# Padding the on-chip tiles that matmuls read to multiples of 128 bytes, in a fused two-block transformer kernel

## The chip, the cores and the metric

The kernel runs on one core of one Trainium2 chip. The metric is the device time of one execution in microseconds, as the median of several runs. The profiled execution, from which all durations here come, is one more run, recorded by the hardware profiler; its own time and its span from the first to the last instruction are given beside the median.

## The reference

Two different transformer blocks are applied one after the other to `x`, 256 tokens of 1024 features, each block two layers deep. All arrays are float32. What matters here is that nearly all the work is matrix products of 256 or 512 token columns with large weight matrices:

```python
# block 1, each of 2 layers
h = rms_norm(x, norm_mix_pre); proj = h @ w_in          # convolution, retention, gated linear attention
x = x + rms_norm(merged @ w_out, norm_mix_post)
f = (silu(h @ w_gate) * (h @ w_up)) @ w_down
x = x + rms_norm(f, norm_ffn_post)
# block 2, each of 2 layers: 256 latent tokens x and 256 context tokens, modulated by silu(c) @ ada_w
mix_x, mix_c = token_mixers(hx, hc, ...)                # conformer convolution, mLSTM, attention
x = x + g1 * mix_x
x = x + g2 * conv_ffn(hx, ffn_w_up, ..., ffn_w_down)    # the context too, in the first layer
```

## The kernel before, in words

Activations are kept with the features on the partitions and the tokens along the row, 128 features to a tile. Weights come from one long stream in DRAM, in the order of use, in chunks of 128 partitions by at most 1024 values (`load`, `chunk`). A float32 product is made from three products of type fp32r: `halve` splits each chunk of weights into a high part `whi` (ScalarE, L197) and a low part `wlo` (VectorE, L199); the activations are split in the same way. `mmT` (L214, L218, L220) then issues high by high, low by high and high by low, with 128 columns of the weights loaded into TensorE and 256 or 512 token columns streamed through (PSUM tiles `pj`, `dn`, `br`). `mmK` (L228, L230, L232) does the reverse where tokens are wanted on the partitions (PSUM tile `pk`): 128 token columns of the activations are loaded and the weights are streamed, 256 columns at a time, or 272 where 16 gate columns ride along (`tok_gates`, `tok_gates_first`). So `whi` and `wlo` are the loaded operand in `mmT` and the streamed one in `mmK`. Small products in plain fp32 (transposes, attention scores, sums of squares, retention and gated attention: `st`, `ro`, `go`, `ms`, `pv` and others) make up the rest; each of those leaves two records in the trace.

All tiles come from pools, laid out in SBUF in the order in which `setup` makes them, each tile rounded up to 32 bytes per partition. The first byte of the constants is 1,152, nine times 128. Where the program's own list of addresses puts the tiles, modulo 128:

| Pool (tile sizes in bytes per partition) | Start modulo 128 | Read by matmuls as |
|---|---|---|
| `pc`, constants: `vecs` 2716, `mats` 512, `sel` 288, `twice` 144, `hb` 96 and others | 0, 32, 64 or 96 | operands of small fp32 products |
| `pw`: `raw`, `whi`, `wlo` (4096) | 64 | weights of all large products |
| `psm`: 11 small tiles (64) | 0 or 64 | column scales in `rsb` |
| `ph`, `pu`, `pt`, `pg` (2048): `hh`, `hl`, `xh`, `xl`, `yl` and most others | 0 | activations |
| `pv`: 5 tiles of 2 x 258 (2064) | 32, 64, 96, 0, 32 | `v` of the mLSTM, some of `yh`, `xh` of `b2_first` |
| `pkc`, `pp`, `pz`, `pg2` (2048, 2304, 1024) | 64 (two of `pg2` at 0) | `kc`, some of `yh`, `fh`, `fl`, `fah`, `fal` |

In a chunk of 272 columns the parts follow each other at 1088 bytes, so they start at 64, 0 and 64. In the stretch at 1537 us the six `yh` tiles of a group lie at 32, 0, 32, 64, 64 and 64, and the six `yl` tiles at 0. By the same list the fp32r matmuls of 256 columns are 10,799 with the streamed operand at 0 and the loaded one at 64; 1,168 with 64 and 0; 1,024 with the streamed one at 32 or 64 (or in the midst of such) and the loaded one at 64; and 24 small ones. Of 512 columns there are 2,368 and 536 with the streamed operand at 0 and not; of 272 columns 288, of 258 columns 64.

The order of the matmuls is the order in which the program issues them; splits and loads run ahead of their use by a priority (`PRE_SPLIT`, `PRE_DMA`), as far as the four buffers of `whi` and `wlo` and the five of `raw` allow.

Of the kernel before, what the change touches and what calls it, by code (L numbers as in the profile page):

```python
# [8 lines left out]
F32 = mybir.dt.float32  # L9
F32R = mybir.dt.float32r  # L10
# [92 lines left out]
class Kern:  # L103
# [84 lines left out]
            (queue or self.nc.sync).dma_start(raw, self.d[stream][at : at + 128 * n].rearrange("(p n) -> p n", p=128))  # L188
        return raw

    def halve(self, raw, n, after=None):

        nc = self.nc
        with self.tc.high_priority(offset=self.PRE_SPLIT):
            hi = self.p_w.tile([128, 1024], F32R, tag="whi", name=self.nm("whi"))[:, 0:n]
            lo = self.p_w.tile([128, 1024], F32R, tag="wlo", name=self.nm("wlo"))[:, 0:n]
            self.high = nc.scalar.activation(hi, raw, AF.Copy)  # L197
            with self.tc.issue_after(after.ins) if after else nullcontext():
                self.mark = nc.vector.tensor_tensor(out=lo, in0=raw, in1=hi.bitcast(F32), op=ALU.subtract)  # L199
        return hi, lo  # L200

    def chunk(self, name, l, r0, kt, c0, width, after=None):
        n = kt * width
        self.ada_beat()
        raw = self.load(self.stream.add(name, l, r0, kt, c0, width), n)
        return [t.rearrange("p (k c) -> p k c", k=kt) for t in self.halve(raw, n, after)]

    def mmT(self, out, w, xh, xl, cs=slice(0, 128), first=True, last=True, mid=None):

# [91 lines left out]
    def setup(self, es):  # L301
        tc, nc, d = self.tc, self.nc, self.d
        MS = bass.MemoryType

        self.PRE_DMA, self.PRE_SPLIT, self.PRE_SOON, self.PRE_NORM = 600, 60, 150, 300
        self.p_c = es.enter_context(tc.tile_pool(name="pc", bufs=1))
        self.p_w = es.enter_context(tc.tile_pool(name="pw", bufs=4))
        self.p_s = es.enter_context(tc.tile_pool(name="psm", bufs=11))
        self.p_h = es.enter_context(tc.tile_pool(name="ph", bufs=12))
        self.p_u = es.enter_context(tc.tile_pool(name="pu", bufs=22))  # L310
        self.p_t = es.enter_context(tc.tile_pool(name="pt", bufs=7))
        self.p_g = es.enter_context(tc.tile_pool(name="pg", bufs=6))
        pool = lambda n, b: es.enter_context(tc.tile_pool(name=n, bufs=b))
        self.p_k = pool("pk", 1)
        self.p_v = pool("pv", 5)
        self.p_kc = pool("pkc", 4)
        self.p_p = pool("pp", 4)
        self.p_z = pool("pz", 2)
        self.p_g2 = pool("pg2", 2)
        self.p_ps = es.enter_context(tc.tile_pool(name="pps", bufs=3, space=MS.PSUM))  # L320
        self.p_aux = es.enter_context(tc.tile_pool(name="paux", bufs=3, space=MS.PSUM))
        self.p_pv = es.enter_context(tc.tile_pool(name="ppv", bufs=2, space=MS.PSUM))
        c = self.p_c
        self.xc = c.tile([128, 8, 512], F32, name="xc")
        self.vecs = c.tile([128, self.vec.n], F32, name="vecs")
        with tc.high_priority(offset=5000):
            for j in range(2):
                nc.sync.dma_start(self.xc[:, 4 * j : 4 * j + 4, 0:256], d["xT"][512 * j : 512 * j + 512].rearrange("(k p) t -> p k t", p=128))
            nc.scalar.dma_start(self.vecs[:, 0:8], d["vecs"][:, 0:8])
            if "b1" in self.parts:  # L330
                self.early = self.load(self.stream.add("w_in", 0, 0, 3, ((GV, 256), (GA, 16)), 272), 816, queue=nc.scalar)
        nc.scalar.dma_start(self.vecs[:, 8:], d["vecs"][:, 8:])
        self.mats = c.tile([128, 128], F32, name="mats")
        nc.scalar.dma_start(self.mats, d["ident"])
        self.ident = self.mats
        self.one256 = c.tile([128, 256], F32, name="one256")
        nc.gpsimd.memset(self.one256, 1.0)
        self.ones = self.one256[:, 0:128]
        self.mhalf = c.tile([128, 16], F32, name="mhalf")
        nc.gpsimd.memset(self.mhalf, -0.5)  # L340
        self.m1024 = c.tile([128, 2], F32, name="m1024")
        nc.gpsimd.memset(self.m1024, 1.0 / 1024)

        self.silu = c.tile([128, 2, 1024], F32, name="silu")
        self.mods = c.tile([128, 2, 48, 2], F32, name="mods")
# [747 lines left out]

    def b2_setup(self):
        nc, d, p = self.nc, self.d, self.p_c
        self.sel = p.tile([16, 2, 36], F32, name="sel")
        nc.scalar.dma_start(self.sel, d["sel"])
        self.cmask = p.tile([128, 2, 128], F32, name="cmask")
        nc.scalar.dma_start(self.cmask, d["cmask"])
        self.twice = p.tile([128, 36], F32R, name="twice")  # L1100
        nc.vector.tensor_tensor(out=self.twice, in0=self.ident[:, 0:36], in1=self.ident[:, 64:100], op=ALU.add)
        self.one1 = self.one256[0:36]
        self.m512 = p.tile([128, 2], F32, name="m512")
        nc.gpsimd.memset(self.m512, 1.0 / 512)
        self.tabs = p.tile([128, 2, 2, 2, 64], F32, name="tabs")
        self.m1 = p.tile([128, 2, 2, 8], F32, name="m1")
        self.hb = p.tile([128, 24], F32, name="hb")
        self.ctx = {}

    def b2_prep(self, l):  # L1110

        nc = self.nc
        V = nc.vector

        for i, (w, sc) in enumerate((("norm1", 8), ("norm2", 32))):
            for s in range(2):
                V.scalar_tensor_tensor(self.m1[:, i, s, :], self.mods[:, l, sc : sc + 8, s], 1.0, self.cols(f"{w}{l}"), ALU.add, ALU.mult)
        V.tensor_scalar(self.hb, self.cols(f"branch_gate_b{l}"), 0.5, None, ALU.mult)

        small = self.u("E")  # L1120
        nc.scalar.dma_start(small[:, 0:508], self.d["prep"][:, l])
        rope = small[:, 0:256].rearrange("p (c t d) -> p c t d", c=2, t=2)
        for i in range(2):
            w = small[:, 256 + 64 * i : 320 + 64 * i]
            V.tensor_tensor(out=self.tabs[:, i, 0], in0=rope[:, 0], in1=w[:, None, :].to_broadcast([128, 2, 64]), op=ALU.mult)
            for a, b in ((0, 32), (32, 0)):
                V.tensor_tensor(out=self.tabs[:, i, 1, :, a : a + 32], in0=rope[:, 1, :, a : a + 32], in1=w[:, None, b : b + 32].to_broadcast([128, 2, 32]), op=ALU.mult)
        V.tensor_scalar(self.tabs[:, 0], self.tabs[:, 0], 0.125, None, ALU.mult)

        k = lambda tag, n: self.p_k.tile([128, n], F32, tag=tag, name=self.nm(tag))  # L1130
        self.hw = k("hw", 124)
        V.tensor_scalar(self.hw, small[:, 384:508], 0.5, None, ALU.mult)
        self.hn = k("hn", 8)
        V.tensor_scalar(self.hn, self.cols(f"mlstm_norm{l}"), 0.5, None, ALU.mult)
        wr = k("wr", 128)
        V.tensor_scalar(wr[:, 0:64], small[:, 256:320], 0.125, None, ALU.mult)
        V.tensor_copy(wr[:, 64:128], small[:, 320:384])
        self.wrow = [wr[:, 0:64], wr[:, 64:128]]
# [435 lines left out]
    def mlstm_kv(self, l, S, h, gates=None):  # L1574


        nc = self.nc
        A = nc.scalar
        k = []
# [1 line left out]
            k.append(self.u("mk"))  # L1581
            A.activation(k[-1], ps, AF.Copy, scale=1.0 / 16)
        v = {}
        new = lambda: self.p_v.tile([128, 2, 258], F32, tag="v", name=self.nm("v"))
        if gates:
            ps = self.tok_gates("w_in_2", l, 3072, 1024 + 3072 + 1024, *self.feats(S), self.mm)
            gates(ps)
# [116 lines left out]
        return self.p_g.tile([128, 512], dt, tag="g", name=self.nm(name))  # L1704

    def vu(self, name, dt=F32):
        return self.p_v.tile([128, 2, 258], dt, tag="v", name=self.nm(name)).rearrange("p a b -> p (a b)")[:, 0:512]

    def b2_mixer(self, l, ahead):

# [164 lines left out]
    def b2_first(self, l, tiles):  # L1875
# [3 lines left out]
        H, L = [], []  # L1879
        with self.tc.high_priority(offset=self.PRE_NORM):  # L1880
            for j in range(4):
                hi = self.p_v.tile([128, 2, 258], F32R, tag="v", name=self.nm("xh"))
                sh = self.mods[:, l, 24 + 2 * j : 26 + 2 * j, 0:1]
                A.activation(hi[:, :, 256:257], sh, AF.Copy)
                V.tensor_tensor(out=hi[:, :, 257:258], in0=sh, in1=hi[:, :, 256:257].bitcast(F32), op=ALU.subtract)
                H += [hi[:, a] for a in range(2)]
                lo = self.bu("xl", F32R)
                L += [lo[:, a * 256 : a * 256 + 256] for a in range(2)]
            for k in range(8):
                A.activation(H[k][:, 0:256], self.xc[:, k, 0:256], AF.Copy, scale=self.m1[:, 1, 0, k : k + 1])  # L1890
            for k in range(8):
                V.scalar_tensor_tensor(L[k], self.xc[:, k, 0:256], self.m1[:, 1, 0, k : k + 1], H[k][:, 0:256].bitcast(F32), ALU.mult, ALU.subtract)
# [304 lines left out]
```

## Time and profile before

| | |
|---|---|
| median of 3 runs (lowest, highest) | 2542.06 us (2538.91, 2551.09) |
| profiled execution, its span | 2540.95 us, 2539.2 us |
| TensorE matmuls busy, weight loads busy | 98%, 91% of the span |
| VectorE, ScalarE, GpSimd busy | 75%, 51%, 6% |
| granted TensorE clock | 0.998 of full speed |

The share of busy time is an average over stages. TensorE's matmuls are pipelined: a record lasts longer than the time to the start of the next one, so how fast they follow each other is read from their starts.

### The profile page before, as it was taken

Reading aid. Unit: us, or ns where it says so; the run is one execution under the profiler, and the core shown is the slowest. Engines: PE = TensorE matmul, PEld = TensorE weight load, DVE = VectorE, ACT = ScalarE, POOL = GpSimd, SP = SyncE. Lnnn points to the kernel's source line nnn. Section 1 sums busy time; section 2 is a strip of 40 time slices with the busy share of each in tenths; the row PEclk is TensorE's granted clock in tenths of the full one; section 3 lists DMA queues with packets and bytes.
Section 4 is the critical chain, followed back from the end, with each engine's and each line's share of the span. In section 5 each row is a group of like instructions: output and inputs, shape, how many; then the busy total and the mean of one; then the engine's idle time right before and its main releaser. Section 6 shows DMA issues by size and latency. Waiting matters only on the chain.

```text
span 2539.2 us, 44691 instructions
## 1 busy us (share of the span) xinstructions
PE 2499.2 (98%) x17998; PEld 2300.5 (91%) x17998; DVE 1916.8 (75%) x3112; ACT 1294.2 (51%) x2027; POOL 156.5 (6%) x167
## 2 busy tenths in 40 slices
PE   8999999999999999999999999999999999999999
PEld 8999999999989998888877779888889999989999
DVE  6998797689879868958864556975687674966994
ACT  6555654654455556234344635642345644675763
POOL 0111000011100000010010110000000000000000
PEclk9999999999999999999999999999999999999999
DMA  6556477445647754232232234434336433444554
GB/s 245 182 204 223 147 268 255 160 174 184 232 142 259 235 172 162 100 100 100 84 118 98 75 125 142 167 122 142 117 133 201 138 100 125 141 134 158 188 189 146
DMA packets 116383, 405.54 MB, mean 160 GB/s; under 512 B 12864, under 2 KB 16704, under 8 KB 116176
## 3 DMA queue, kind: packets, MB, share of 16 engines
q1 hardware_dynamic: 113344, 399.01, 47.0%
q10 hardware_dynamic: 2832, 3.68, 0.5%
q8 instruction: 141, 2.31, 0.4%
q14 instruction: 66, 0.54, 0.1%
HBM read 401.59 MB, written 1.05 MB: 159 GB/s over the span
## 4 chain that ended last, share of the span: by engine, by line
PE 82%; DVE 9%; issue 5%; ACT 2%; DMA 1%; POOL 1%; ACTq 0%; DVEq 0%; SPq 0%; POOLq 0%
PE pj L214 19%; PE pj L218 19%; PE pj L220 19%; PE dn L218 3%; PE dn L220 3%; PE dn L214 3%; DVE wlo L199 2%; DVE dw L1306 2%; PE pv L1675 2%; PE pk L228 1%; PE pk L232 1%; PE pk L230 1%; PE ms L1635 1%; PE br L214 1%; PE br L220 1%
## 5 line engine op out<-in xcount | busy, mean ns | idle before, releaser
L199 DVE TENSOR_TENSOR wlo<-raw,whi 128x1024 fp32r<-128x1024 f32 (+3 forms) x674 | 813.9, 1214 | 332.4 <-ACT whi L197 325.8
L197 ACT ACTIVATE whi<-raw 128x1024 fp32r<-128x1024 f32 (+3 forms) x674 | 697.6, 1040 | 548.6 <-PE pj L220 242.7
L214 PE MATMUL pj<-hh,whi 128*128 128x256 f32 (+1 forms) x3088 | 520.8, 310 | 1.7 <-ACT whi L197 1.0
L218 PE MATMUL pj<-hh,wlo 128*128 128x256 f32 (+1 forms) x3088 | 512.1, 307 | 1.1 <-DVE wlo L199 1.1
L214 PEld LDWEIGHTS pj<-hh,whi 128*128 128x128 f32 x3088 | 431.5, 188 | 40.9 <-ACT hh L1176 2.5
L218 PEld LDWEIGHTS pj<-hh,wlo 128*128 128x128 f32 x3088 | 427.9, 188 | 36.7 <-issue 2.5
L220 PE MATMUL pj<-hl,whi 128*128 128x256 f32 (+1 forms) x2408 | 382.5, 295 | 0.0
L220 PEld LDWEIGHTS pj<-hl,whi 128*128 128x128 f32 x2408 | 323.3, 188 | 17.7 <-issue 0.3
L373 DVE CUSTOM_DVE_ANT_0 adr<-raw,silu 128x1024 bf16<-128x1024 f32 x192 | 243.4, 1270 | 0.7
L220 PE MATMUL pj<-kc,whi 128*128 128x512 f32 (+1 forms) x680 | 151.2, 344 | 0.0
L1306 DVE SCALAR_TENSOR_TENSOR dw<-z,hw,dw 128x512 f32<-128x512 f32 (+1 forms) x240 | 135.9, 610 | 0.1
L220 PEld LDWEIGHTS pj<-kc,whi 128*128 128x128 f32 x680 | 111.9, 188 | 16.7
L1862 ACT ACTIVATE fc<-pj,vecs 128x256 f32<-128x256 f32 (+1 forms) x78 | 52.0, 667 | 112.9 <-PE pj L220 109.7
L228 PE MATMUL pk<-whi,hh 128*128 128x256 f32 (+1 forms) x512 | 86.7, 288 | 0.0
L230 PE MATMUL pk<-wlo,hh 128*128 128x256 f32 (+1 forms) x512 | 83.0, 281 | 1.2 <-DVE wlo L199 1.2
L1863 DVE SCALAR_TENSOR_TENSOR fc<-pj,vecs,fc 128x255 f32<-128x255 f32 (+1 forms) x78 | 47.4, 609 | 48.8 <-ACT fc L1862 48.0
L214 PE MATMUL dn<-fah,whi 128*128 128x256 f32 (+1 forms) x440 | 76.8, 301 | 0.7 <-DVE xc L1941 0.7
L218 PE MATMUL dn<-fah,wlo 128*128 128x256 f32 (+1 forms) x440 | 76.5, 300 | 0.9 <-DVE wlo L199 0.9
L220 PE MATMUL dn<-fal,whi 128*128 128x256 f32 (+1 forms) x440 | 76.4, 300 | 0.1
L228 PEld LDWEIGHTS pk<-whi,hh 128*128 128x128 f32 x512 | 71.5, 188 | 2.7 <-issue 1.1
L214 PE MATMUL pj<-yh,whi 128*128 128x256 f32 (+1 forms) x384 | 71.9, 314 | 0.0
L230 PEld LDWEIGHTS pk<-wlo,hh 128*128 128x128 f32 x512 | 70.1, 188 | 1.6 <-DVE wlo L199 1.5
(432 smaller groups left out, 3625.4 us busy)
## 6 DMA issues: line engine op xcount, KB each, us to landing
raw<-stream SPq DMA_DIRECT2D x620, 512.0 KB, 3.6
raw<-ada_stream SPq DMA_DIRECT2D x96, 512.0 KB, 3.4
raw<-stream SPq DMA_DIRECT2D x36, 384.0 KB, 3.3
raw<-stream SPq DMA_DIRECT2D x11, 408.0 KB, 3.7
raw<-stream SPq DMA_DIRECT2D x6, 272.0 KB, 2.8
xc<-xT SPq DMA_DIRECT2D x2, 512.0 KB, 5.6
silu<-c SPq DMA_DIRECT2D x2, 512.0 KB, 6.7
xc<-cT ACTq DMA_DIRECT2D x1, 1024.0 KB, 12.9
```

What stands on the lines that cost most here:

```text
L197: self.high = nc.scalar.activation(hi, raw, AF.Copy)
L199: self.mark = nc.vector.tensor_tensor(out=lo, in0=raw, in1=hi.bitcast(F32), op=ALU.subtract)
L214: mm(out, wh[:, k, cs], xh[k], start=first and k == 0, stop=False)
L218: mm(out, wl[:, k, cs], xh[k], start=False, stop=False)
L220: mm(out, wh[:, k, cs], xl[k], start=False, stop=last and k == kt - 1)
L228: mm(out, xh[k], wh[:, k, :], start=first and k == 0, stop=False)
L230: mm(out, xh[k], wl[:, k, :], start=False, stop=False)
L373: nc.vector.tensor_tensor_reduce(junk, raw, self.silu[:, s], 0.5, 0.0, ALU.mult, ALU.add, self.mods[:, l, n, s : s + 1])
L1306: V.scalar_tensor_tensor(d, src, w, d, ALU.mult, ALU.add)
L1675: T.matmul(pv[dr][:, 0:257], a, b, start=q_ == 0, stop=q_ == len(todo) - 1)
L1862: A.activation(v(t), v(ps), AF.Identity, scale=w(1), bias=self.col(f"ffn_conv_b{l}", f + i))
L1863: V.scalar_tensor_tensor(v(t)[..., 1:256], v(ps)[..., 0:255], w(0), v(t)[..., 1:256], ALU.mult, ALU.add)
```

## The change

Every pool's and every constant's size is made a multiple of 128 bytes, so that every tile, and every slice of 128 or 256 columns of one, begins at such a multiple. A chunk of 272 weight columns is split into rows at a pitch of 288. `psm` gets a twelfth buffer, three small constants share a tile, and the memset of `m512` moves from `b2_setup` to `setup`. The core of the diff, with the padded sizes:

```diff
-    def halve(self, raw, n, after=None):
+    def halve(self, raw, kt, width, after=None):
         nc = self.nc
+        n = kt * -(-width // 32) * 32
+        rows = lambda t: t.rearrange("p (k c) -> p k c", k=kt)
         with self.tc.high_priority(offset=self.PRE_SPLIT):
             hi = self.p_w.tile([128, 1024], F32R, tag="whi", name=self.nm("whi"))[:, 0:n]
             lo = self.p_w.tile([128, 1024], F32R, tag="wlo", name=self.nm("wlo"))[:, 0:n]
+            if width % 32:
+                hi, lo, raw = rows(hi)[:, :, 0:width], rows(lo)[:, :, 0:width], rows(raw)
...
-        return [t.rearrange("p (k c) -> p k c", k=kt) for t in self.halve(raw, n, after)]
+        hl = self.halve(raw, kt, width, after)
+        return hl if width % 32 else [t.rearrange("p (k c) -> p k c", k=kt) for t in hl]
...
-        self.p_s = es.enter_context(tc.tile_pool(name="psm", bufs=11))
+        self.p_s = es.enter_context(tc.tile_pool(name="psm", bufs=12))
...
-        self.vecs = c.tile([128, self.vec.n], F32, name="vecs")
+        self.vecs = c.tile([128, -(-self.vec.n // 32) * 32], F32, name="vecs")[:, 0 : self.vec.n]
...
-        self.mhalf = c.tile([128, 16], F32, name="mhalf")
+        small = c.tile([128, 32], F32, name="small")
+        self.mhalf, self.m1024, self.m512 = small[:, 0:16], small[:, 16:18], small[:, 18:20]
...
-        self.sel = p.tile([16, 2, 36], F32, name="sel")
+        self.sel = p.tile([16, 96], F32, name="sel")[:, 0:72].rearrange("p (a c) -> p a c", a=2)
-        self.twice = p.tile([128, 36], F32R, name="twice")
+        self.twice = p.tile([128, 64], F32R, name="twice")[:, 0:36]
-        self.hb = p.tile([128, 24], F32, name="hb")
+        self.hb = p.tile([128, 32], F32, name="hb")[:, 0:24]
...
-        k = lambda tag, n: self.p_k.tile([128, n], F32, tag=tag, name=self.nm(tag))
+        k = lambda tag, n: self.p_k.tile([128, -(-n // 32) * 32], F32, tag=tag, name=self.nm(tag))[:, 0:n]
...
-        new = lambda: self.p_v.tile([128, 2, 258], F32, tag="v", name=self.nm("v"))
+        new = lambda: self.p_v.tile([128, 2, 288], F32, tag="v", name=self.nm("v"))
...
-                hi = self.p_v.tile([128, 2, 258], F32R, tag="v", name=self.nm("xh"))
+                hi = self.p_v.tile([128, 2, 288], F32R, tag="v", name=self.nm("xh"))
...
-                H += [hi[:, a] for a in range(2)]
+                H += [hi[:, a, 0:258] for a in range(2)]
```

## Rows read from the trace of the kernel before

**Rows 1.** The page: busy us of each engine (share of the span) and instructions.

```profile
PE 2499.2 (98%) x17998; PEld 2300.5 (91%) x17998; DVE 1916.8 (75%) x3112; ACT 1294.2 (51%) x2027; POOL 156.5 (6%) x167
```

**Rows 2.** The page: the chain that ended last, share of the span by engine.

```profile
PE 82%; DVE 9%; issue 5%; ACT 2%; DMA 1%; POOL 1%; ACTq 0%; DVEq 0%; SPq 0%; POOLq 0%
```

**Rows 3.** Two windows: length, busy time of each engine (instructions), granted clock, DMA share, GB/s.

```profile
320.00:380.00 60.00, 60.00 (x532) 60.00 (x531) 54.98 (x72) 29.99 (x35) 0.00 (x0) 1.00 0.79 269
...
1016.00:1079.00 63.00, 62.38 (x356) 54.49 (x355) 61.52 (x109) 18.17 (x31) 2.12 (x8) 1.00 0.30 101
```

**Rows 4.** Timeline of TensorE from 320 us: start, us, engine, line, names, count.

```profile
320.26 1.07 PE L218 MATMUL pj<-hh,wlo 128*128 128x256 f32 x8
...
324.80 1.07 PE L214 MATMUL pj<-hh,whi 128*128 128x256 f32 x8
```

**Rows 5.** Timeline of TensorE from 1537 us: aligned yl after unaligned yh.

```profile
1537.27 0.87 PE L214 MATMUL pj<-yh,whi 128*128 128x256 f32 x6
1537.97 0.87 PE L218 MATMUL pj<-yh,wlo 128*128 128x256 f32 x6
1538.68 0.84 PE L220 MATMUL pj<-yl,whi 128*128 128x256 f32 x6
1539.36 0.87 PE L214 MATMUL pj<-yh,whi 128*128 128x256 f32 x6
```

**Rows 6.** Timeline of TensorE from 1074 us, weights streamed; four matmuls to a group.

```profile
1074.14 0.63 PE L232 MATMUL pk<-whi,hl 128*128 128x256 f32 x4
...
1076.97 0.64 PE L232 MATMUL pk<-whi,kc 128*128 128x256 f32 x4
```

**Rows 7.** Groups of TensorE, whole span: names, shape, count | busy us, mean ns | idle before.

```profile
L220 PE MATMUL pj<-hl,whi 128*128 128x256 f32 x2032 | 279.1, 277 | 0.0
L220 PE MATMUL pj<-hl,whi 128*128 128x512 f32 x376 | 103.4, 396 | 0.0
L220 PE MATMUL pj<-kc,whi 128*128 128x512 f32 x376 | 102.3, 393 | 0.0
...
L220 PE MATMUL pj<-kc,whi 128*128 128x256 f32 x304 | 48.9, 283 | 0.0
...
L232 PE MATMUL pk<-whi,hl 128*128 128x256 f32 x272 | 43.0, 279 | 0.0
...
L232 PE MATMUL pk<-whi,kc 128*128 128x256 f32 x176 | 28.0, 281 | 0.0
```

**Rows 8.** Timeline of TensorE from 188.6 us, fp32, weights S at 0.

```profile
188.61 1.05 PE L1062 MATMUL go<-gv,S 128*128 128x128 f32 x8
...
190.39 0.39 PE L1064 MATMUL go<-gv,S 128*128 128x128 f32 x2
```

**Rows 9.** Timeline of TensorE from 120 us, fp32, weights rp at 64.

```profile
119.99 1.27 PE L1046 MATMUL ro<-rv,rp 128*128 128x128 f32 x10
...
121.33 0.39 PE L1046 MATMUL ro<-rv,rp 128*128 128x128 f32 x2
```

**Rows 10.** Timeline of TensorE from 1046 us, 512 columns.

```profile
1046.06 2.02 PE L214 MATMUL pj<-hh,whi 128*128 128x512 f32 x8
...
1049.78 1.10 PE L220 MATMUL pj<-hl,whi 128*128 128x512 f32 x4
```

**Rows 11.** The fp32 run of ms: its timeline at 1071 us, and its group.

```profile
1071.47 1.89 PE L1635 MATMUL ms<-mq,mk 128*128 128x256 f32 x8
...
L1635 PE MATMUL ms<-mq,mk 128*128 128x256 f32 x160 | 37.8, 379 | 0.0
```

**Rows 12.** Timeline of TensorE from 939.7 us, 272 columns.

```profile
939.71 0.54 PE L228 MATMUL pk<-whi,hh 128*128 128x272 f32 x3
...
940.83 0.54 PE L228 MATMUL pk<-whi,hh 128*128 128x272 f32 x3
```

**Rows 13.** Groups of the splits of 816 columns.

```profile
L199 DVE TENSOR_TENSOR wlo<-raw,whi 128x816 fp32r<-128x816 f32 x12 | 12.0, 1003 | 14.7 <-ACT whi L197 14.7
L197 ACT ACTIVATE whi<-raw 128x816 fp32r<-128x816 f32 x12 | 10.5, 882 | 7.1 <-PE dn L220 4.5 <-DMA raw<-stream 1.5 <-PE pk L232 1.1
```

More of the change, by code (lines that the diff above doesn't have):

```diff
@@ L338, in setup @@
         self.ones = self.one256[:, 0:128]
-        self.mhalf = c.tile([128, 16], F32, name="mhalf")
+        small = c.tile([128, 32], F32, name="small")
+        self.mhalf, self.m1024, self.m512 = small[:, 0:16], small[:, 16:18], small[:, 18:20]
         nc.gpsimd.memset(self.mhalf, -0.5)
-        self.m1024 = c.tile([128, 2], F32, name="m1024")
         nc.gpsimd.memset(self.m1024, 1.0 / 1024)
+        nc.gpsimd.memset(self.m512, 1.0 / 512)
         self.silu = c.tile([128, 2, 1024], F32, name="silu")
@@ L1099, in b2_setup @@
         nc.scalar.dma_start(self.cmask, d["cmask"])
-        self.twice = p.tile([128, 36], F32R, name="twice")
+        self.twice = p.tile([128, 64], F32R, name="twice")[:, 0:36]
         nc.vector.tensor_tensor(out=self.twice, in0=self.ident[:, 0:36], in1=self.ident[:, 64:100], op=ALU.add)
         self.one1 = self.one256[0:36]
-        self.m512 = p.tile([128, 2], F32, name="m512")
-        nc.gpsimd.memset(self.m512, 1.0 / 512)
         self.tabs = p.tile([128, 2, 2, 2, 64], F32, name="tabs")
         self.m1 = p.tile([128, 2, 2, 8], F32, name="m1")
-        self.hb = p.tile([128, 24], F32, name="hb")
+        self.hb = p.tile([128, 32], F32, name="hb")[:, 0:24]
         self.ctx = {}
@@ L1706, in vu @@
     def vu(self, name, dt=F32):
-        return self.p_v.tile([128, 2, 258], dt, tag="v", name=self.nm(name)).rearrange("p a b -> p (a b)")[:, 0:512]
+        return self.p_v.tile([128, 2, 288], dt, tag="v", name=self.nm(name)).rearrange("p a b -> p (a b)")[:, 0:512]
     def b2_mixer(self, l, ahead):
```

## Prediction

> **What bounds the kernel now.** I read the share of busy time first [rows 1]: the matmuls fill 2499.2 of 2539.2 us and the weight loads 2300.5, with VectorE at 1916.8 behind them. The chain that ended last [rows 2] says the same of the path: 82% of the span lies on TensorE, 9% on VectorE. A change to matmul spacing is therefore felt nearly at its own size. The two windows [rows 3] show where it may not be: from 320 to 380 us TensorE is busy all of the 60 us and VectorE 54.98, so VectorE has some 8% in hand; from 1016 to 1079 us VectorE is busy 61.52 of 63 us and has 2%. The granted clock is 1.00 in both, the 2.4 GHz level, so the clock is not in question.
>
> Nothing in the change touches how many matmuls there are or how wide they are. All that can move is the time from the start of one matmul to the start of the next, which I call its spacing. It is read in the timeline from the starts of consecutive groups; a duration is no spacing, since a matmul's record runs on while the next has begun, but in dense runs the two differ by a constant, so differences between mean durations are differences between spacings.
>
> **What the trace says about alignment today.** The tile addresses stand in the table ahead. Four kinds of fp32r matmul of 256 columns can be compared, by where the streamed operand and the loaded weights start, modulo 128 bytes.
> - Streamed at 0, weights at 64 (10,799 of them, the bulk): 40 matmuls from 320.26 to 324.80 us [rows 4], 4.54 / 40 = 113.5 ns. The yl group of six further on takes 0.68 us, 113.3 ns [rows 5]. I use 113.4.
> - Streamed at 64, weights at 0 (1,168, all in the pk groups, where the split weight is what streams): 24 from 1074.14 to 1076.97 us [rows 6], 2.83 / 24 = 117.9 ns.
> - Streamed off 128, weights at 64 (1,024): the two yh groups beside yl, 12 in 1.41 us, 117.5 ns [rows 5]; their tiles lie at 32, 0, 32, 64, 64 and 64. The kc groups have a mean duration of 283 ns where hl, the same loop over aligned tiles, has 277 [rows 7]: 6 more, 119.4. I use 118.5.
> - Both at 0: none exists, and that is what the change makes of nearly all.
>
> So the start of the streamed tile costs 4 to 6 ns a matmul; yh and yl alternate in one loop with one set of weights, which leaves no other reason. What the start of the weights costs is not shown at a streamed start of 0. The nearest rows are with the weight tiles streamed: pk over kc (stationary at 64) has 281 ns, pk over hl (stationary at 0) 279 [rows 7], so 2 ns. Two other rows bound it. In the fp32 runs of 128 columns, go loads weights at 0 and needs 1.78 us for 16, 111.3 ns [rows 8]; ro loads weights at 64 and needs 1.34 us for 12, 111.7 ns [rows 9]. First, these are equal, so in that stream the start of the weights costs nothing. Second, this looks like the least time for a load of 128 weight columns, and none of the fp32r runs in these rows is quicker. I take 111.5 as the floor under a matmul of 256 columns.
>
> **The parts.**
> - (A) The bulk gets aligned weights: 113.4 less 111.5 is 1.9 ns, times 10,799: 20.5 us. Bounds: 0 by go and ro; a loss is in the rivals. I take the full 1.9, because the 2 ns in pk are at the same streamed width and type.
> - (B) The pk groups stream at 0: 117.9 less 111.5 is 6.4 ns, times 1,168: 7.5 us; 5.3 us if the bulk stays at 113.4.
> - (C) kc, yh, fh, fah and xl in the odd pools: 118.5 less 111.5 is 7.0 ns, times 1,024: 7.2 us; 5.2 us at 113.4.
> - (D) 512 columns: hh and hl run 16 in 1049.78 less 1046.06, 3.72 us, 232.5 ns [rows 10]. Here the streamed start does no harm: kc at 64 with weights at 64 has 393 ns, hl at 0 with weights at 64 has 396 [rows 7]. I take 2 ns for the weights again on the 2,368 aligned ones, 4.7 us, and nothing on the 536 others. Bounds: 0, and the fp32 run of ms, both operands at 0: eight in 1.89 us with a duration of 379, (1890 - 379) / 7 = 215.9 ns for as long a stream at half the rate [rows 11]. That would be 16.6 ns each.
> - (E) The 272-column groups: nine in 940.83 less 939.71 us, 124.4 ns, with starts alternating between 64, 0 and 64 [rows 12]. The starts at 0 are not quicker, so a pitch of 288 gains about nothing here; with the few 257s and 258s, 0.5 us, between 0 and 1.
> - The split of these chunks now writes rows of 272 at a pitch of 288. It has the same 816 or 544 elements per partition; 12 splits of 816 take 1003 ns on VectorE and 882 on ScalarE [rows 13], the rest are shorter. Each row might add a start-up; were it a tenth, 36 operations by 0.1 us is under 4 us of engines that have time, beside some 24 matmuls of work per chunk: nothing on the path, 1 us if it fell in the nearly full window of [rows 3].
> - The twelfth small buffer, the padded constants and the earlier memset of m512 add no instruction and no wait. A buffer more can only come free sooner. Nothing is moved past a queue apart from that one memset on GpSimd. Price zero; the cover is GpSimd's 156.5 us of work in the span [rows 1].
>
> **The sum.** 20.5 + 7.5 + 7.2 + 4.7 + 0.5 = 40.4 us of TensorE time. If only the chain's 82% counts, 33; if all of it, 40.4. VectorE's 2% in the crowded window and ScalarE's splits, which wait for buffers the matmuls free, will take some of it back; I take 36. The profiled execution is 2540.95 us (2539.2 of span and 1.75 around it), 1.1 below the median of 2542.06: 2540.95 - 36 = 2505, own range 2490 to 2520.
>
> **The rivals.**
> - Only the streamed operand counts. Then A and D are nothing, B and C 5.3 + 5.2 = 10.5: 2530. For it: go and ro. Against it: the 2 ns in pk.
> - Nothing counts, 2541. The Trainium skill, "SBUF — State Buffer", section Specifications (TRN2), gives 16-byte cachelines and a penalty for crossing to a new line; by that rule every start at a multiple of 32 bytes is as good as one at 128. The trace disagrees: yh at 32 and 64 needs 117.5 ns where yl needs 113.3 [rows 5].
> - All stalls go. If the 20 ns or so by which 512 columns exceed 215.9 come from the weights' start too, D becomes about 2,368 x 16.6 + 536 x 16 = 48 us, with A to C 83: 2540.95 less nine tenths of that is 2466. The Trainium skill, "TensorE: Matmul & The Clock Gate", section Back-to-back issue gap, gives N / 2.4 + 2.5 ns, 215.8 for 512 columns and 109.2 for 256, so by that page such a stall needs a reason. For this rival: the stall exists only in fp32r. Against it: at 512 columns the worst aligned pair is the quicker one, and 272 columns stall with everything at 0.
> - Slower: the two streams collide. Weights and streamed tile would now always start at the same place modulo 128; today only the (64, 64) groups do, and they are the slowest. If what costs is the equal place and not the odd one, the bulk goes from 113.4 to 118.5, 5.1 ns by 10,799: +55, less the 4.7 of the 512s: 2591; with 2 ns instead, 22 less 5: 2558. It decides from 1.0 ns on, where it eats B and C. Against it: (0, 64) and (64, 0) are the same distance apart and differ by 4.5 ns, so the streamed start counts by itself.
>
> **Chances.** Forecast 0.42; all stalls go 0.18; only the streamed operand 0.19; nothing 0.05; collision 0.16. The range from 2458 to 2550 holds the first and the two middle ones, the greater part of the quick rival and little of the collision: about 0.8. A difference of 0.5%, 12.7 us, is what a measurement of this kernel can tell from no change: faster by more than that is the forecast and the quick rival, 0.60; within it the streamed-only and the null case, 0.24; slower 0.16.
>
> **What would show it.** In a window of dense work like [rows 4], 40 matmuls should take 4.46 us instead of 4.54; the pk and kc groups should have the mean duration of hl; yh and yl should take the same time per six; the 512s should drop by about 2 ns. If hl stays at 277 and only pk and kc drop, the first rival holds. If hl rises towards 283, the collision does. The prediction is wrong if the floor of 111.5 does not hold for fp32r loads, if the spacing at 512 moves by more than 5 ns, or if VectorE becomes the releaser of matmuls where it now has 2% in hand.

## The result, and the profile after

The changed kernel is slower. Its median is 2585.19 us (2582.90 to 2586.91, 4 runs) against 2546.57 us (2538.91 to 2552.20, 4 runs) for the kernel before, a ratio of 1.014 with a 95% interval from 1.0115 to 1.0164. The profiled execution took 2584.33 us with a span of 2582.6, 43.4 us more than the span of before, at the same granted clock of 0.998. The forecast of 2505 us, its range up to 2550 and its sign were all wrong; the time came out near the 2591 of the fourth rival, the collision.

The page first: busy time by engine, then the chain that ended last by engine, to be held against [rows 1, 2].

```profile
PE 2546.6 (99%) x17998; PEld 2361.6 (91%) x17998; DVE 1923.0 (74%) x3112; ACT 1292.9 (50%) x2027; POOL 153.9 (6%) x167
...
PE 81%; DVE 8%; issue 6%; ACT 2%; DMA 1%; POOL 1%; ACTq 0%; SPq 0%; DVEq 0%; POOLq 0%
```

The same instructions, and TensorE alone has grown: matmuls by 47.4 us, weight loads by 61.1. VectorE's 6 us more are small beside that, and ScalarE and GpSimd have less. The path is still TensorE's.

The two windows (length, busy time of PE, PEld, DVE, ACT and POOL with instructions, granted clock, DMA share, GB/s), against [rows 3]:

```profile
320.00:380.00 60.00, 60.00 (x502) 60.00 (x502) 54.16 (x70) 28.42 (x34) 0.00 (x0) 1.00 0.75 248
1016.00:1079.00 63.00, 62.47 (x347) 53.48 (x346) 54.14 (x103) 28.03 (x51) 4.97 (x8) 1.00 0.37 126
```

In the dense window TensorE never rests in either kernel, but it gets through 502 matmuls where it got through 532. So each one takes longer; nothing waits.

The timeline of TensorE from 320 us (start, us, engine, line, names, count), against [rows 4]:

```profile
320.06 1.12 PE L224 MATMUL pj<-hh,wlo 128*128 128x256 f32 x8
...
324.86 1.12 PE L220 MATMUL pj<-hh,whi 128*128 128x256 f32 x8
```

40 matmuls in 4.80 us are 120.0 ns each, where 113.5 had stood. And from the timeline at 1567 us, against [rows 5]:

```profile
1566.99 0.88 PE L220 MATMUL pj<-yh,whi 128*128 128x256 f32 x6
1567.70 0.88 PE L224 MATMUL pj<-yh,wlo 128*128 128x256 f32 x6
1568.42 0.88 PE L226 MATMUL pj<-yl,whi 128*128 128x256 f32 x6
1569.14 0.88 PE L220 MATMUL pj<-yh,whi 128*128 128x256 f32 x6
```

`yh` and `yl` have become equal, as forecast, but not because `yh` fell to `yl`: `yl` rose from 0.68 to 0.72 us for six. The groups over the whole span (count | busy us, mean ns of one | idle before), against [rows 7]:

```profile
L226 PE MATMUL pj<-hl,whi 128*128 128x256 f32 x2032 | 292.4, 284 | 0.0
L226 PE MATMUL pj<-kc,whi 128*128 128x512 f32 x376 | 102.4, 393 | 0.0
L226 PE MATMUL pj<-hl,whi 128*128 128x512 f32 x376 | 101.2, 390 | 0.0
L226 PE MATMUL pj<-kc,whi 128*128 128x256 f32 x304 | 48.9, 283 | 0.0
L238 PE MATMUL pk<-whi,hl 128*128 128x256 f32 x272 | 43.7, 283 | 0.0
L238 PE MATMUL pk<-whi,kc 128*128 128x256 f32 x176 | 27.8, 279 | 0.0
```

`hl` at 256 columns goes from 277 to 284 ns, past the 283 of `kc`; `hl` at 512 goes from 396 to 390. Two parts of one change pull against each other. The order of the matmuls is the same in both kernels, so every record can be set beside its partner. Summing the time from each start to the next by kind, short idle times included, gives the table below. Regular pools are those at 0 modulo 128 in the table of pools ahead; the odd pools are `pv`, `pkc`, `pp`, `pz` and `pg2`.

| Kind of matmul | Count | Before, us | After, us | Difference |
|---|---|---|---|---|
| bulk, 256 columns, both operands in the regular pools | 10,767 | 1279.7 | 1335.2 | +55.5 |
| `pk` over regular tiles, weights streamed | 1,168 | 144.0 | 145.1 | +1.1 |
| 256 columns with one operand in the odd pools | 1,080 | 131.1 | 130.9 | -0.2 |
| 512 columns, regular pools | 2,352 | 560.9 | 549.3 | -11.6 |
| 512 columns, odd pools | 552 | 130.3 | 130.9 | +0.6 |
| 272 columns | 288 | 41.3 | 41.4 | +0.1 |
| 257 and 258 columns | 336 | 65.0 | 63.4 | -1.6 |
| fp32, the rest | 1,454 | 182.0 | 181.8 | -0.2 |

The differences add up to 43.7 us, and the spans differ by 43.4. Nearly the whole loss is in the bulk, 5.2 ns a matmul.

### The profile page after: what moved, and what is told of

Its sections match the earlier page's. It is cut to its first block, busy times and chain, and to the rows that moved or that the text cites. A ratio compares the mean times of both kernels' runs of the same rounds, so it can differ in the third digit from the quotient of the medians.

```text
span 2582.6 us, 44683 instructions
## 1 busy us (share of the span) xinstructions
PE 2546.6 (99%) x17998; PEld 2361.6 (91%) x17998; DVE 1923.0 (74%) x3112; ACT 1292.9 (50%) x2027; POOL 153.9 (6%) x167
## 4 chain that ended last, share of the span: by engine, by line
PE 81%; DVE 8%; issue 6%; ACT 2%; DMA 1%; POOL 1%; ACTq 0%; SPq 0%; DVEq 0%; POOLq 0%
PE pj L220 19%; PE pj L224 19%; PE pj L226 18%; PE dn L224 3%; PE dn L226 3%; PE dn L220 3%; PE pk L234 2%; PE pk L236 2%; PE pk L238 2%; DVE wlo L204 2%; PE pv L1680 1%; DVE dw L1311 1%; PE br L220 1%; PE br L226 1%; PE br L224 1%
## 5 line engine op out<-in xcount | busy, mean ns | idle before, releaser
L220 PE MATMUL pj<-hh,whi 128*128 128x256 f32 (+1 forms) x3088 | 529.3, 313 | 1.5 <-ACT whi L202 0.8
L224 PE MATMUL pj<-hh,wlo 128*128 128x256 f32 (+1 forms) x3088 | 522.7, 310 | 1.1 <-DVE wlo L204 1.1
L220 PEld LDWEIGHTS pj<-hh,whi 128*128 128x128 f32 x3088 | 442.2, 190 | 38.8 <-ACT hh L1181 2.5
L224 PEld LDWEIGHTS pj<-hh,wlo 128*128 128x128 f32 x3088 | 442.1, 191 | 32.2 <-issue 2.5
L226 PE MATMUL pj<-hl,whi 128*128 128x256 f32 (+1 forms) x2408 | 393.6, 300 | 0.0
L226 PEld LDWEIGHTS pj<-hl,whi 128*128 128x128 f32 x2408 | 336.3, 192 | 15.5 <-issue 0.3
L1868 DVE SCALAR_TENSOR_TENSOR fc<-pj,vecs,fc 128x255 f32<-128x255 f32 (+1 forms) x78 | 47.4, 609 | 48.2 <-ACT fc L1867 48.1
```

What stands on the lines that cost most here:

```text
L220: mm(out, wh[:, k, cs], xh[k], start=first and k == 0, stop=False)
L224: mm(out, wl[:, k, cs], xh[k], start=False, stop=False)
L226: mm(out, wh[:, k, cs], xl[k], start=False, stop=last and k == kt - 1)
L1868: V.scalar_tensor_tensor(v(t)[..., 1:256], v(ps)[..., 0:255], w(0), v(t)[..., 1:256], ALU.mult, ALU.add)
```

## The experiments

**The theories.** The trace shows that the bulk got slower, not why. Three readings were open. First, the place of the weights counts by itself, and 0 modulo 128 bytes is a bad place for them. Second, the distance between the two operands counts: the start of the loaded tile less the start of the streamed one. In the kernel before, by the program's addresses, that is 64 in the bulk; in the changed kernel it is 0. Third, the finished layout has nothing to do with it. The distance needs a modulus: the addresses of before put the bulk at 64, `pk` over regular tiles at 192, and the odd pools mostly at 128, all modulo 256; the changed kernel has 0, 0 and 128.

Two pads move things without touching an instruction: one ahead of the constants shifts constants and weights by x bytes, and one of y bytes ahead of the pool `ph`, with x + y = 512 (256 in the run on the kernel before), puts everything behind it back in place modulo 256. In the texts below, "the kernel before" has the median of the runs made on the same chip beside it. Where one time is given, the kernel ran once; the kernel before alone ranged from 2538.91 to 2552.76 us, so a single run tells nothing below some 14 us, and the spacings carry the argument. They are means over the matmuls that nothing held up.

**The weights moved by 64** (on the changed kernel), so that the bulk is at a distance of 64 again:

```diff
+        es.enter_context(tc.tile_pool(name="padb", bufs=1)).tile([128, 112], F32, name="padb")
         self.p_h = es.enter_context(tc.tile_pool(name="ph", bufs=12))
...
+        c.tile([128, 16], F32, name="pada")
         self.xc = c.tile([128, 8, 512], F32, name="xc")
```

> The changed kernel, with constants and weight tiles moved up by 64 bytes and every other tile by 512, so that only the weights start off 128 again. Spacing of the bulk (256 fp32r columns over hh, hl and the like): in the changed kernel 119.9 ns. Place theory (a tile off 128 costs, whatever the other does): no lower than 119.9, and worse for pk, where the moved tile streams. Distance theory (what counts is where the loaded operand starts relative to the streamed one, modulo 256): bulk back at a distance of 64, 113.4 ns; 512 columns from about 227 back to 233; pk, then at a distance of 192, 117.6 instead of 119.7. Time by the distance theory 2584 - 55 + 12 - 3 = about 2538.

Measured: 2546.41 us, with 2544.71 for the kernel before. The bulk falls from 119.8 to 115.4 ns and the 512s rise from 228.0 to 233.4: one offset of 64 bytes takes back the gain at 512 columns and most of the loss at 256 (the bulk stood at 114.2 in the kernel before and was expected at 113.4 here; what is missing comes up under the two levels). All the rest of the change (the pitch of 288, the padded value tiles, the twelfth buffer, the moved memset) is still in this kernel, and together it is worth less than one run can tell from zero. Groups over the whole span:

```profile
L226 PE MATMUL pj<-hl,whi 128*128 128x256 f32 x2032 | 282.1, 278 | 0.0
L226 PE MATMUL pj<-hl,whi 128*128 128x512 f32 x376 | 103.4, 396 | 0.0
```

These are the 277 and 396 of [rows 7] again, nearly.

**The weights moved by 128 and by 256**, with pads of 32 and 96 and of 64 and 64 columns:

```diff
-        c.tile([128, 16], F32, name="pada")
+        c.tile([128, 32], F32, name="pada")
...
-        ....tile([128, 112], F32, name="padb")
+        ....tile([128, 96], F32, name="padb")
```

> The same with weights moved by 128 bytes: every tile still starts at a multiple of 128. Place theory, and a distance theory modulo 128: nothing changes, 2584, bulk 119.9. Distance theory modulo 256: the bulk stands at 128 as the kc groups do in both kernels, irregular spacings around 119, 512 columns 231 instead of 227 (2368 x 4 = +9 us), while kc and the pp tiles come to a distance of 0: 2584 to 2594.

> Weights moved by 256 bytes. Distance theory modulo 256, modulo 128 and place theory: nothing changes, 2584, bulk 119.9, 512 columns 227 to 228. Only a distance that counts modulo 512 or more would show here.

Measured: 2576.51 us at 128, with 118.75 ns in the bulk and 232.6 in the 512s; 2588.24 us at 256, with 119.8 and 228.0. The second is the changed kernel over again, to 0.1 ns in both widths, so from 0 the pattern repeats after 256 bytes. At 128, which is as aligned as 0 by the measure the change goes by, the 512s lose their gain.

**Everything moved by 64**, weights and activations alike: the pad ahead of the constants alone.

```diff
+        c.tile([128, 16], F32, name="pada")
         self.xc = c.tile([128, 8, 512], F32, name="xc")
```

> All tiles, constants, weights and activations alike, moved by 64 bytes: everything starts off 128, all distances stay. Place theory: the streamed start off 128 costs, bulk above 119.9 by 2 to 6 ns, 20 to 60 us more. Distance theory: nothing changes, 2584, bulk 119.9, 512 columns 227 to 228.

Measured: 2582.44 us; 119.8 ns in the bulk and 228.0 in the 512s. Groups of this kernel:

```profile
L226 PE MATMUL pj<-hl,whi 128*128 128x256 f32 x2032 | 291.7, 283 | 0.0
L226 PE MATMUL pj<-hl,whi 128*128 128x512 f32 x376 | 101.2, 390 | 0.0
```

This run carries the most. Every tile that matmuls read starts at 64 modulo 128, which the change set out to abolish, and the times are those of the fully aligned kernel. The first reading falls: with the distance held at 0, a move of every place by 64 bytes made no difference.

**Distances of 32 and 96** (the weight pad 8 and 24 columns, the other 120 and 104):

```diff
+        c.tile([128, 8], F32, name="pada")
...
+        ....tile([128, 120], F32, name="padb")
```

> The changed kernel with weights moved by 32 bytes, so that the bulk stands at a distance (loaded minus streamed start, modulo 256) of 32 and the pk groups over hh and hl at 224. If slots of 64 bytes are what counts, the bulk is like the one at 0, 119.8 ns, and pk like the one at 192, 117.6; if the distance counts byte by byte, values between: bulk between 113.4 and 119.8. Time 2540 to 2590. Place theory was refuted by the first four runs and has no forecast here.

> The same with weights moved by 96: bulk at a distance of 96, pk at 160. Slots of 64 bytes: bulk like that at 64, 113.4 to 115.4 ns, time about 2546; byte by byte: between 113.4 and the irregular 118.8 of 128, time 2545 to 2577.

Measured: 2578.94 and 2582.34 us, with 2546.02 for the kernel before; 118.3 and 118.6 ns in the bulk, 232.9 and 234.0 in the 512s. Neither neighbour of 64 is better than 128 by more than half a nanosecond. That is no slope with its best near 64; of the distances tried so far, 64 stands alone.

**All 256-column kinds towards 64.** To the first experiment a pad of 128 bytes ahead of the pool `pv` is added, so that the odd pools also stand at 64 from the weights.

```diff
+        pool("padc", 1).tile([128, 32], F32, name="padc")
```

> The changed kernel with weights 64 bytes up and with the kc, pp and value tiles brought to the same place modulo 256 as hh and hl, so that every product with loaded weights stands at a distance of 64. Distance theory: bulk 113.4 to 114.2 ns, kc and pp groups from 118.4 to 113.4 to 115 (some 1000 matmuls by 4 ns, 4 us), pk stays at 117: about 2536 to 2542. If instead the bulk of the run with weights at 64 was disturbed by something else than its neighbours at 192, it stays at 115.4.

Measured: 2540.41 us. `kc` in `mmT` goes from 118.4 ns in the first experiment to 115.2, the bulk stands at 114.6. Groups:

```profile
L226 PE MATMUL pj<-hl,whi 128*128 128x256 f32 x2032 | 280.5, 277 | 0.0
...
L226 PE MATMUL pj<-kc,whi 128*128 128x256 f32 x304 | 47.5, 278 | 0.0
```

`kc` is now as quick as `hl`, 278 beside 277. It moved by 128 bytes, from a multiple of 128 to another, so its alignment by the change's measure is what it was; its distance went from 192 to 64. In [rows 7] its 283 had been the prediction's evidence for the streamed start.

**The kernel before, with its weights moved to distance 0** and nothing else of the change:

```diff
+        es.enter_context(tc.tile_pool(name="padb", bufs=1)).tile([128, 16], F32, name="padb")
...
+        c.tile([128, 48], F32, name="pada")
```

> The kernel before, with nothing of the change but the weights' place: constants and weights moved by 192 bytes, everything else by 256, so that weights and hh, hl stand at a distance of 0 and kc and pp, unaligned as before, at 64. Distance theory: bulk 119.8 as in the changed kernel (+55 to +59 us), 512 columns 227 (-12), kc and pp down to about 114 (-5), pk 119.7 (+2): about 2584 against 2541, with none of the padding. If the padding itself or the pitch of 288 were to blame, 2541.

Measured: 2581.80 us against 2546.02. Groups:

```profile
L220 PE MATMUL pj<-hl,whi 128*128 128x256 f32 x2032 | 291.8, 283 | 0.0
L220 PE MATMUL pj<-hl,whi 128*128 128x512 f32 x376 | 101.2, 391 | 0.0
```

So the distance of the bulk alone does what the whole change does: 119.8 ns in the bulk, 228.3 in the 512s, and the 36 us. One reading of this run did not fit a simple table of distances, though. The tiles of the odd pools in `mmT`, `kc` and others, now mostly stood at 64 and still took 118.1 ns, while the weights streamed over `kc` stood at 192 and took only 114.1. In the kernel before, `pk` over regular tiles at the same 192 takes 117.6.

**A place by use.** Since, of the distances tried, 256 columns are best at 64 and 512 columns at 0, the weights can be put where their user wants them. This is built on the kernel before: the weight tiles get 64 more columns, and each chunk starts at an offset that its user names.

```diff
+    place = ALONE = 16
+    STREAM, WIDE = 48, 0
...
-            hi = self.p_w.tile([128, 1024], F32R, tag="whi", name=self.nm("whi"))[:, 0:n]
+            hi = self.p_w.tile([128, 1088], F32R, tag="whi", name=self.nm("whi"))[:, self.place : self.place + n]
...
-    def chunk(self, name, l, r0, kt, c0, width, after=None):
+    def chunk(self, name, l, r0, kt, c0, width, after=None, place=None):
+        self.place = self.ALONE if place is None else place
...
-            w = self.chunk(name, l, s * 512, 4, c0, 256)
+            w = self.chunk(name, l, s * 512, 4, c0, 256, place=self.STREAM)
...
-            w = self.chunk(name, l, 0, 4, c0, 256)
+            w = self.chunk(name, l, 0, 4, c0, 256, place=self.WIDE)
```

The offsets are 16 columns (64 bytes) where 256 columns are streamed over loaded weights, 48 columns (192 bytes) where the weights are streamed themselves, which is a distance of 64 again, and 0 where 512 columns are streamed. A twelfth small buffer and a pad of 64 bytes put the odd pools in line with the others.

> The kernel before with the split weights placed by their use inside wider tiles (1088 columns): 64 bytes past the activations where 256 token columns stream over loaded weights, 64 short of them where the weights stream, level with them where 512 columns stream; kc and pp brought level with hh. Distance theory: bulk 113.4 to 114.5 ns, kc and pp groups down from 119 to about 115 (1000 by 4 = 4 us), pk from 117.6 to 114 to 116 (1168 by 2 to 3.5 = 3 us), 512 columns from 233 to 228 (2840 by 5 = 14 us): 21 us less than before, ratio 0.992. If the distance only mattered for the bulk, or the gain came back as waits on the splits, 1.000.

Measured: 2526.76 us (2524.05 to 2532.07, 6 runs) against 2548.83 (2543.99 to 2552.76, 11 runs), a ratio of 0.9918 with an interval from 0.9904 to 0.9932. This beats both kernels. Page and groups:

```profile
PE 2483.4 (98%) x17998; PEld 2300.6 (91%) x17998; DVE 1917.2 (76%) x3112; ACT 1293.3 (51%) x2027; POOL 156.1 (6%) x167
...
L224 PE MATMUL pj<-hl,whi 128*128 128x256 f32 x2032 | 280.7, 277 | 0.0
L224 PE MATMUL pj<-hl,whi 128*128 128x512 f32 x376 | 101.2, 390 | 0.0
L224 PE MATMUL pj<-kc,whi 128*128 128x512 f32 x376 | 100.8, 390 | 0.0
L224 PE MATMUL pj<-kc,whi 128*128 128x256 f32 x304 | 47.4, 278 | 0.0
L236 PE MATMUL pk<-whi,hl 128*128 128x256 f32 x272 | 42.4, 278 | 0.0
```

Each of these groups of 256 columns is at 277 or 278 and each of 512 at 390, at or below the better of both kernels in its row of [rows 7]; only `hl` at 256, at 277 already, gains nothing. By the same sums as in the table above, the 512s give back 13.1 + 1.3 us, the odd pools and `pk` 3.3, and the bulk takes 3.2 more than before, which the two levels below explain. The profiled executions, from which these sums come, differ by 15.2 us; the medians differ by 22.

**Finer steps around 64**, in the same kernel: offsets of 12, 52 and 0 for a distance of 48, and of 20, 44 and 0 for 80.

```diff
-    place = ALONE = 16
-    STREAM, WIDE = 48, 0
+    place = ALONE = 12
+    STREAM, WIDE = 52, 0
```

> The same with 48 bytes in place of 64, for loaded and for streamed weights. With a sharp best distance the bulk rises towards the 118.3 of 32 (some +40 us); with a plateau from 48 to 80 it stays at 114. 512 columns stay at a distance of 0 and at 228.

> The same with 80 bytes in place of 64. Sharp: bulk towards the 118.6 of 96; plateau: 114. 512 columns at 228.

Measured: 2573.55 us and 119.2 ns at 48; 2567.59 us and 118.8 ns at 80. The 512s, at 0 in both, keep their 227.4. Sixteen bytes to either side lose the quick spacing wholly. Between these two runs and the one before nothing moves but the split weights, so the constants and small tiles that the earlier pads had moved along are not the cause.

**Two levels at 64.** What did not fit in the run with the weights of before at 0 made me look at the spread in place of the mean. Cutting the records into stretches of eight successive matmuls of one distance, nine in ten stretches at 64 fall at 113 or at 118 ns, and those at the distances of the table where none is quick lie at 117 to 121 ns (at 48, at 116.5 to 123.5):

| Kernel | Distance | Stretches | of them below 113.5 ns | of them from 117.5 to 118.5 ns |
|---|---|---|---|---|
| before | 64 | 1,178 | 925 | 129 |
| before | 192 | 119 | 2 | 112 |
| weights at 64 | 64 | 1,183 | 591 | 467 |
| weights at 64 | 192 | 139 | 30 | 106 |
| all kinds towards 64 | 64 | 1,333 | 878 | 343 |
| place by use | 64 | 1,456 | 908 | 430 |
| place by use, 48 instead | 48 | 1,460 | 0 | 980 |
| place by use, 80 instead | 80 | 1,463 | 0 | 93 |
| weights at 128 | 128 | 1,306 | 0 | 481 |
| changed kernel | 0 | 1,302 | 0 | 46 |

So the distance decides whether the quick level exists, and something else whether a stretch is in it. The timeline of the first experiment shows one such fall:

```profile
296.24 1.07 PE L226 MATMUL pj<-xl,whi 128*128 128x256 f32 x8
...
298.76 1.21 PE L224 MATMUL pj<-xh,wlo 128*128 128x256 f32 x8
299.80 1.11 PE L226 MATMUL pj<-xl,whi 128*128 128x256 f32 x8
...
300.98 1.11 PE L224 MATMUL pj<-xh,wlo 128*128 128x256 f32 x8
301.92 1.11 PE L226 MATMUL pj<-xl,whi 128*128 128x256 f32 x8
```

The group at 296.24 is quick: it is followed at 297.15, eight in 0.91 us, 113.8 ns. The one at 298.76 is disturbed once: 1.04 us to the next start. From there on the groups take 0.94 us, 117.5 ns, and they stay so for some 900 matmuls, past the place of [rows 4]. The same group in the kernel before was not disturbed:

```profile
299.18 1.07 PE L218 MATMUL pj<-xh,wlo 128*128 128x256 f32 x8
300.09 1.07 PE L220 MATMUL pj<-xl,whi 128*128 128x256 f32 x8
...
302.13 1.07 PE L220 MATMUL pj<-xl,whi 128*128 128x256 f32 x8
303.04 1.07 PE L214 MATMUL pj<-xh,whi 128*128 128x256 f32 x8
```

0.91 us throughout. This is why the place by use did not gain in the bulk: 908 of 1,456 stretches were quick, against 925 of 1,178. What decides between the levels is not a larger modulus: in that run, stretches wholly at 64 modulo 512 were quick in 201 of 320 cases and those wholly at 320 in 196 of 288.

The run by use has a second kind of fall, with no wait in it. Its timelines of matmuls and of weight loads (PEld) where `pk` hands over to `pj`:

```profile
51.08 0.62 PE L234 MATMUL pk<-wlo,hh 128*128 128x256 f32 x4
51.53 0.62 PE L236 MATMUL pk<-whi,hl 128*128 128x256 f32 x4
51.99 1.10 PE L218 MATMUL pj<-hh,whi 128*128 128x256 f32 x8
52.93 1.10 PE L222 MATMUL pj<-hh,wlo 128*128 128x256 f32 x8
...
51.88 0.89 PEld L218 LDWEIGHTS pj<-hh,whi 128*128 128x128 f32 x7
```

Four matmuls take 0.45 us, the next four 0.46, and then eight take 0.94, 117.5 ns each. The weights of the first `pj` matmul load from 51.88 us on, while the last `pk` matmul still streams. By the program's addresses those two tiles are 128 apart, though each product by itself stands at 64. All five hand-overs that were reached at the quick level, and had no wait, ended it (in the fifth, from `dn` to `pk`, the two tiles are 0 apart); of two reached at the slow level one led back to the quick one. The other four falls inside unbroken stretches of this run follow a matmul held up for 237 to 946 ns, as the one above follows a disturbance. So the distance that counts seems to be that of the next loaded tile to the one still streaming; no run moved that distance alone.

**The other side.** 192 is 64 the other way round, and the table has a few quick stretches there. The last run gives the kernel with a place by use its two places exchanged:

```diff
-    place = ALONE = 16
-    STREAM, WIDE = 48, 0
+    place = ALONE = 48
+    STREAM, WIDE = 16, 0
```

> The kernel of the run by use with the two places exchanged, so that its 256-column matmuls stand at a distance of 192 bytes (64 the other way) instead of 64; the 512-column ones stay at 0. In the traces so far, stretches of eight matmuls fall at two levels at 64, 113 and 118 ns; at 192 nearly all lie at 118 (112 of 119 in the kernel before), but the weights streamed over kc in the run that moved the weights of the kernel before stood at 192 and took 114.1. If the sign of the distance counts, and 64 alone has the quick level, the bulk takes 117.5 ns and, with 12,400 matmuls 2.7 ns above the run by use, the time is 2560 us. If 64 to either side will do, the bulk has stretches at 113 ns for at least a third of its length and the time is 2525 to 2545 us. If the distance is not what counts but the place of the weights themselves, nothing singles out this place: 118.5 to 120 ns and 2570 to 2580 us.

Measured: 2554.62 us, with 2544.55 for the kernel before, and 117.5 ns over some 12,500 matmuls. 95 stretches of 1,457 are below 113.5, 1,355 lie from 117.5 to 118.5, and there is next to nothing between. Groups:

```profile
L224 PE MATMUL pj<-hl,whi 128*128 128x256 f32 x2032 | 286.5, 279 | 0.0
L224 PE MATMUL pj<-hl,whi 128*128 128x512 f32 x376 | 101.2, 390 | 0.0
```

The sign counts, as the first reading of that run had it, though not quite in its form: the quick level exists at 192 as well, but a stretch is rarely in it (7%, against 50 to 79% at 64).

## Why the prediction was wrong

**What held.** TensorE is the bound and spacing is felt at its full size: the sum over matmuls, 43.7 us, is the span's 43.4. VectorE did not become the releaser in the crowded window; its 61.52 us of [rows 3] are 54.14 in the same window, which holds fewer matmuls. The splits at a pitch of 288, priced at nothing, cost nothing, here against [rows 13]:

```profile
L204 DVE TENSOR_TENSOR wlo<-raw,whi 128x816 fp32r<-128x816 f32 x12 | 12.0, 1003 | 15.0 <-ACT whi L202 15.0
L202 ACT ACTIVATE whi<-raw 128x816 fp32r<-128x816 f32 x12 | 10.5, 880 | 7.3 <-PE dn L226 4.7 <-DMA raw<-stream 1.3 <-PE pk L238 1.3
```

1003 and 880 ns for what took 1003 and 882. The twelfth buffer, the constants and the memset brought no new wait. The 272-column groups (E) were given 0.5 us and moved by 0.1.

**The step that failed: "(0, 64) and (64, 0) are the same distance apart and differ by 4.5 ns, so the streamed start counts by itself."** With it the collision was dismissed, and A, B and C, which count each start by itself, rest on it. It goes wrong twice. The modulus was 128, because that was the change's measure; modulo 256, which no row had been read for, the two distances are 64 and 192. And the 4.5 ns between them is no property of a place: both have the quick level, and the bulk was mostly in it and `pk` nearly never (925 of 1,178 stretches, 2 of 119). When the weights alone moved by 64 from the changed kernel, the bulk went from 119.8 ns to 115.4; when weights and tiles moved by 64 together, it stayed at 119.8, to 0.1 ns. In place of A's gain of 1.9 ns a matmul the change brought a loss of 5.2, because it took the bulk from a distance of 64 to 0.

**"yh and yl alternate in one loop with one set of weights, which leaves no other reason."** It leaves one: with the weights fixed, moving the streamed tile changes its distance too. `yl` stood at 64, the six tiles of `yh` at 160, 192, 32, 0, 128 and 128. The comparison [rows 5] changed two quantities at once, and so did `kc` against `hl` [rows 7].

**(A) +20.5 us of gain became 55.5 of loss.** The floor of 111.5 ns came from fp32 rows [rows 8, 9], and no fp32r stream reached it at any distance tried; 113.3 is the quickest level in all the kernels of this study. The 2 ns "for the weights' start" between `pk` over `hl` and over `kc` [rows 7] were 192 against 128, once more a distance. The chosen end of A's range was the wrong one for another reason as well: its lower bound was 0 "by go and ro", and the loss was handed to the rivals with a chance of 0.16, when the kernel before held no fp32r matmul at all with both operands at 0. A state of which no row exists was counted as the best of the states seen.

**(B) 7.5 us and (C) 7.2 us became -1.1 and 0.2.** `pk` went from 192 to 0, 117.6 to 119.7 ns. The odd pools mostly stayed at 128, since weights and tiles moved together: 119.0 and 119.3 ns.

**(D) 4.7 us became 11.6.** The sign was right; the term was mis-sized, 4.9 ns each in place of 2, because the 2 were borrowed from `pk`. The quick rival's 16.6 did not come: the 512s at distance 0 need 228.0 ns, still 12 above the fp32 run of [rows 11].

**The rivals.** The collision gave 2591 us out of 5.1 ns by 10,799 less 4.7; measured were 5.2 ns, less 11.6. Its price was therefore right, in part by luck, since the 5.1 came from groups at a distance of 128 and not 0, and its reason only half: an equal start is one of the many bad distances, and not the only one, since 32, 48, 80, 96 and 128 are within 1.5 ns of it. What stands out is not the 0 but the 64, where alone of the distances tried the quick level is common. By the prediction's own sign it was the collision: `hl` rose to 284 ns, past the 283 named there. "Only the streamed operand" and "nothing" are both excluded by the runs that moved the weights alone.

**What stays open.** Why 64 bytes, why modulo 256, and what arbitrates between the two operands: no row shows it. What drops a stretch out of the quick level, and what brings it back, was seen in the traces and not varied. Why 512 columns want distance 0 was not pursued either. The small groups of four of the odd pools sometimes carried on at the level of their neighbours in place of their own; there were too few for a verdict.

## What to carry to other kernels

Where TensorE is the bound, look at where the loaded and the streamed operand lie relative to each other (here modulo 256 bytes) before aligning either; an offset of 64 bytes in one pool moved this kernel by 1.4%, and the better offset was a different one for 256 columns than for 512. If two operands are compared by one of them changing place, the distance has changed too, so that no conclusion about a place follows until both have been moved together. A layout of which the trace holds no example is an unknown with two signs, and it is priced first by a pad of a few bytes, which costs one run.

## What the runs showed of the hardware

The spacing of fp32r matmuls depends on the distance of their operands' starts modulo 256 bytes (loaded less streamed). Means over undisturbed matmuls, ns:

| Distance | 0 | 32 | 48 | 64 | 80 | 96 | 128 | 192 |
|---|---|---|---|---|---|---|---|---|
| 256 columns, bulk | 119.8 | 118.3 | 119.2 | 114.2 to 115.4 | 118.8 | 118.6 | 118.75 | 117.4 |
| 512 columns, regular pools | 227.4 to 228.3 | 232.9 | not run | 233.3 | not run | 234.0 | 232.6 | not run |

The smaller groups of the odd pools do not all follow the table: 256 columns took 118.1 ns at 64 and 114.1 at 192 in the kernel before with its weights at 0, and 512 columns took 230.3 at 0 with the weights moved by 128 and 229.4 at 192 with the weights moved by 64.

At 64, and seldom at 192, 256 columns run at one of two levels, about 113.3 or 117.8 ns, for hundreds of matmuls on end; in the kernel with a place by use, all stretches at the quick level would be worth (114.8 - 113.3) x 12,500 = 19 us more, an estimate from these rows. The order and the shapes of the matmuls are the same in all these runs, and the granted clock is 1.00 in the dense window of before and of after.

The Trainium skill, "TensorE: Matmul & The Clock Gate", section Step-by-step: what each phase is for, says that TensorE reads SBUF by two independent ports, one for the streamed operand and one for the weights, and that loading the next weights takes no read bandwidth from the running matmul. The trace disagrees in this much: 113.3 to 119.8 ns for the same instructions in the same order, by nothing but where one operand starts in relation to the other.
